# Layer 1 attention: the high and low halves of the queries stacked on the partitions

## The chip, the cores and the metric

The kernel runs on one core of one Trainium2 chip. The metric is the device time of one execution in microseconds (us). Before the change it is 1184.41 us, the median of three runs (1181.78 to 1184.94). The profile used below was taken of one further execution, which took 1183.15 us.

The engines are named as the profile names them: PE is TensorE (matrix products), PEld its loading of weights, DVE is VectorE, ACT is ScalarE, POOL is GpSimd and SP is SyncE, which issues the DMAs.

## The reference

Two decoder layers over 512 tokens of width 1024 in float32. Each layer has an attention mixer and a SwiGLU feed-forward block, both behind an RMS norm that is scaled and shifted by a condition. The change touches the mixer of layer 1 alone: sliding-window attention with 16 query heads of 64 elements, 4 key heads, a window of 128 and one learned sink per head. Cut to that:

```
q, k, v = _split_cols(h @ w_in, ODD_SIZES)              # 16 x 64, 4 x 64, 4 x 64
q = _rms_norm(q.reshape(b, s, C_HEADS, HEAD_DIM), qn_c)
k = _rms_norm(k.reshape(b, s, C_KV_HEADS, HEAD_DIM), kn_c)
...
logits = einsum('bnqhgd,bnkhd->bnhgqk', qb, kk) * HEAD_DIM ** -0.5   # band: own and previous block
logits = logits - slope * dist                                       # masked outside the window
p = softmax(concatenate([logits, sink]))[..., :-1]
out = einsum('bnhgqk,bnkhd->bnqhgd', p, vv)
```

The tokens are worked in four blocks of 128 queries. A block sees its own and the previous block's keys, 256 in all; block 0 sees only its own 128.

## The kernel before

Nearly all products run in the number type that the kernel calls FR, in which an operand is carried as two tiles: `hi`, a rounded copy, and `lo`, what the rounding left out. A product of two such operands is three matrix products into one accumulator: hi by hi, hi by lo and lo by hi (`mm3`). Every instruction is issued through a few helpers, so the profile's lines are those of the helpers: L434 is every matrix product (`mms`), L445 every transpose on PE (`tr`), L460 every ACT pass (`act`, `copy`), L476 every DVE or POOL operation on two tensors (`tt`), L496 the fused pass that scales the logits, adds the distances and takes the row minimum (`ttmin`), and L484 a multiplication by a scalar.

The order of the work is not the order of the code. Each helper hands an operation, with an estimate of its duration, to a list scheduler (`Sched`), which places the operations of all engines by dependencies, free buffers and priority; in up to eight rounds it sets new due times for DVE and keeps the shortest plan. The instructions are then emitted in that order, and each engine works through its own list in order. One call of `mms` is one operation for the scheduler: its products stand next to each other. For an FR product of n columns the estimate is 0.4219 ns times n, at least 107 ns, whatever part of the array it uses.

Layer 1 goes through `odd`. One chunk of weights gives keys and values. The keys of each of the 4 key heads are transposed to tiles `ckT` of 128 partitions by 512 tokens, and the head's 64 rows stand in them twice, in partitions 0 to 63 and again in 64 to 127. Then, for two groups of 8 query heads (`hg`), the four blocks of queries are projected (`proj_f`, 24 products of 512 columns with weights and activations in FR), normalised and transposed (`q_t`), and attended (`attn_c`). A transposed query tile has 4 column groups of 128 queries; each holds an even head in partitions 0 to 63 and the odd head beside it in 64 to 127. `split_out` makes of it the tiles `hi` and `lo` with one ACT pass and one DVE pass over 128 x 512.

`attn_c` makes the logits head by head: three products with 64 rows, in the head's own half of the partitions. The tiles of logits are PSUM buffers of the tag `lg`, two at a time besides what the scheduler grants as next in line, and `ttmin` on DVE empties them. The scheduler fills the gaps of the attention with the projections of the following blocks, and of the output product at the end.

Of the kernel before, what the change touches and what calls it, by code (L numbers as in the profile page):

```python
# [10 lines left out]
F = mybir.dt.float32  # L11
FR = mybir.dt.float32r
AF = mybir.ActivationFunctionType
OP = mybir.AluOpType
# [3 lines left out]
P = 128  # L18
# [22 lines left out]
def f32(v):  # L41
    return float(np.float32(v))
# [330 lines left out]
class Kern:  # L373
# [442 lines left out]
            self.copy(hi, src, scale=gain)  # L816
            self.stt(lo, src, gain, hi.bitcast(F), OP.mult, OP.subtract)

    def q_t(self, ps, qs):

        qf = self.t2("qf")
        r = self.head_rstd(ps, 8)
        self.tt(r, r, qs, OP.mult, e="POOL")
        self.tt(qf.rearrange("p (h d) -> p h d", d=64), ps.rearrange("p (h d) -> p h d", d=64),
                r[:, :, None].to_broadcast([P, 8, 64]), OP.mult)
        tp = self.ps("tp")
        for j in range(4):
            self.tr(tp[:, j * P:(j + 1) * P], qf[:, j * P:(j + 1) * P])
        hi, lo = self.t2("q", dt=FR), self.t2("q", dt=FR)
        self.split_out(tp, hi, lo)  # L830
        return [t.rearrange("p (a b) -> p a b", a=4) for t in (hi, lo)]


# [120 lines left out]
    def attn_c(self, i, hg, q, Y):  # L954

        b0 = max(i - 1, 0)
        nb = i + 1 - b0
        n = nb * P
        dsl = self.Dc[:, 256 - n:256]
        nm, sums, rec, es = (self.sm() for _ in range(4))  # L960
        pv = self.ps("pv")
        T = []
        for hp in range(4):
            t = self.t2("L")
            for e in range(2):
                h = 2 * hp + e
                r = slice(64 * e, 64 * e + 64)
                kh, kl = self.ckT[(8 * hg + h) // 4]
                ks = slice(b0 * P, b0 * P + n)
                lg = self.logits(q[0][r, hp], q[1][r, hp], kh[r, ks], kl[r, ks], n)  # L970
                self.ttmin(t[:, e * 256:e * 256 + n], lg[:, :n], dsl, f32(SL_C[8 * hg + h]), nm[:, h:h + 1])
                T.append((t, e * 256))
        hs = slice(8 * hg, 8 * hg + 8)
        self.tt(nm, nm, self.nsink[:, hs], OP.min)
        self.tt(es, nm, self.sinks[:, hs], OP.add, e="POOL")
        self.act(es, es, AF.Exp)
        for h, (t, c) in enumerate(T):
            self.act(t[:, c:c + n], t[:, c:c + n], AF.Exp, scale=-1.0, bias=nm[:, h:h + 1], accum=sums[:, h:h + 1])
        self.tt(sums, sums, es, OP.add)
        self.recip(rec, sums)  # L980
        for h, (t, c) in enumerate(T):
            self.ts(t[:, c:c + n], t[:, c:c + n], rec[:, h:h + 1], None, OP.mult)
        self.pv_t(pv, T, [[(t, c + b * P) for t, c in T] for b in range(nb)],
                  [tuple(self.cv[b0 + b][:, (2 * hg + g) * 64:(2 * hg + g) * 64 + 64] for g in range(2)) for b in range(nb)])
        self.y_out(pv, Y, i)
# [109 lines left out]
    def odd(self, H):  # L1095
        self.ckT = [(self.t2("k", dt=FR), self.t2("k", dt=FR)) for _ in range(4)]
        self.cv = []
        w = self.chunk()
        for i in range(NB):
            ps = self.proj_f(H, i, w, 512, "st")  # L1100
            t = self.t2("v")
            self.copy(t[:, 0:256], ps[:, 256:512])
            self.cv.append(t)
            r = self.head_rstd(ps[:, 0:256], 4)
            qf = self.k_t(ps[:, 0:256], r[:, 0:4], 4, True)
            tp = self.ps("tp")
            for j in range(4):
                self.tr(tp[:, j * P:(j + 1) * P], qf[:, j * P:(j + 1) * P])
            sl = slice(i * P, (i + 1) * P)
            for j in range(4):  # L1110
                self.split_out(tp[:, j * P:(j + 1) * P], self.ckT[j][0][:, sl], self.ckT[j][1][:, sl], self.gain[:, 2:3])
        ys = []
        for hg in range(2):
            w = self.chunk()
            Y = self.new_y()
            for i in reversed(range(NB)):
                ps = self.proj_f(H, i, w, 512)
                q = self.q_t(ps, self.qs[:, 16 + 8 * hg:24 + 8 * hg])
                self.attn_c(i, hg, q, Y)
            ys += Y  # L1120
        return ys
# [253 lines left out]
```

## Time and profile before

| | before |
|---|---|
| median of three runs | 1184.41 us |
| profiled execution | 1183.15 us, its span 1181.3 us |
| busy PE / PEld / DVE / ACT / POOL | 1158.7 / 995.8 / 903.3 / 604.6 / 85.3 us |
| mean granted clock of PE | 0.996 |
| PE in the chain that ended last | 86% |
| attention of layer 1, about 690 to 800 us from the start | 110 us |

The span runs from the first to the last instruction; 1.85 us lie around it. A busy time is the time in which at least one instruction of an engine runs. For PE it says little: the ends of matrix products are modelled, a product of 256 columns is listed with about 0.28 us although the next one starts 0.11 us later. What PE takes for a piece of work is therefore read from the starts of its instructions. In the names of forms, `64*128 64x256` is a product with 64 rows and 128 columns of weights and an operand of 256 columns that streams by; `128*128` uses all rows.

### The profile page before, as it was taken

Reading aid. Unit: us, or ns where it says so; the run is one execution under the profiler, and the core shown is the slowest. Engines: PE = TensorE matmul, PEld = TensorE weight load, DVE = VectorE, ACT = ScalarE, POOL = GpSimd, SP = SyncE. Lnnn points to the kernel's source line nnn. Section 1 sums busy time; section 2 is a strip of 40 time slices with the busy share of each in tenths; the row PEclk is TensorE's granted clock in tenths of the full one; section 3 lists DMA queues with packets and bytes.
Section 4 is the critical chain, followed back from the end, with each engine's and each line's share of the span. In section 5 each row is a group of like instructions: output and inputs, shape, how many; then the busy total and the mean of one; then the engine's idle time right before and its main releaser. Section 6 shows DMA issues by size and latency. Waiting matters only on the chain.

```text
span 1181.3 us, 19707 instructions
## 1 busy us (share of the span) xinstructions
PE 1158.7 (98%) x7648; PEld 995.8 (84%) x7648; DVE 903.3 (76%) x1976; ACT 604.6 (51%) x1396; POOL 85.3 (7%) x224
## 2 busy tenths in 40 slices
PE   6989999999999999999999999999999999999998
PEld 3867677679989988899989876668999988999988
DVE  6589999846998889889984866756999843788831
ACT  5564266854745522355533647664856521556510
POOL 0132223300000000000000111100000000000000
PEclk9999999999999999999999999999999999999999
DMA  9634614202244469634362231112123332133411
GB/s 350 247 135 175 220 68 146 72 1 72 72 170 151 162 235 334 250 143 148 138 234 105 72 107 37 72 37 72 72 80 103 139 125 72 72 108 108 161 37 36
DMA packets 32430, 151.78 MB, mean 128 GB/s; under 512 B 3152, under 2 KB 4304, under 8 KB 21072
## 3 DMA queue, kind: packets, MB, share of 16 engines
q1 hardware_dynamic: 32336, 150.52, 35.8%
q8 instruction: 60, 0.98, 0.3%
q14 instruction: 34, 0.28, 0.1%
HBM read 148.41 MB, written 2.10 MB: 127 GB/s over the span
## 4 chain that ended last, share of the span: by engine, by line
PE 86%; DVE 5%; ACT 1%; POOL 0%; issue 0%
PE ps L434 82%; PE ps L445 3%; DVE t L911 1%; DVE t L491 1%; DVE sm L910 1%; DVE w L476 1%; ACT t L460 0%; DVE t L476 0%; POOL sm L476 0%; DVE t L496 0%; DVE sm L502 0%; DVE t L484 0%; ACT sm L460 0%; POOL sm L484 0%; DVE sm L491 0%
## 5 line engine op out<-in xcount | busy, mean ns | idle before, releaser
L434 PE MATMUL ps<-t,w 128*128 128x256 f32 (+2 forms) x5520 | 821.5, 310 | 0.5 <-ACT t L460 0.4
L434 PEld LDWEIGHTS ps<-t,w 128*128 128x128 f32 x5520 | 751.9, 191 | 57.5 <-issue 6.2
L460 ACT ACTIVATE w<-raw 128x512 fp32r<-128x512 f32 (+1 forms) x364 | 225.3, 663 | 160.7 <-PE ps L434 92.6
L476 DVE TENSOR_TENSOR w<-raw,w 128x512 fp32r<-128x512 f32 (+1 forms) x340 | 244.6, 749 | 58.0 <-PE ps L434 43.0
L460 ACT ACTIVATE t<-ps 128x256 f32<-128x256 f32 (+6 forms) x376 | 151.0, 430 | 206.6 <-PE ps L434 145.7
L434 PE MATMUL ps<-w,t 128*128 128x512 f32 (+1 forms) x768 | 189.4, 390 | 0.1
L434 PEld LDWEIGHTS ps<-w,t 128*128 128x128 f32 x768 | 133.3, 190 | 35.2 <-issue 9.7
L476 DVE TENSOR_TENSOR t<-t,t 128x256 f32<-128x256 f32 (+3 forms) x159 | 81.6, 538 | 16.1 <-ACT t L460 15.7
L476 DVE TENSOR_TENSOR t<-ps,t 128x256 f32<-128x256 f32 (+4 forms) x188 | 73.7, 415 | 23.1 <-ACT t L460 12.2
L491 DVE SCALAR_TENSOR_TENSOR x<-ps,mod,x 128x512 f32<-128x512 f32 (+1 forms) x64 | 39.4, 615 | 66.2 <-PE ps L434 65.9
L434 PE MATMUL ps<-t,t 64*128 64x256 f32 (+5 forms) x592 | 86.2, 356 | 1.0 <-ACT t L460 0.5
L434 PEld LDWEIGHTS ps<-t,t 64*128 64x128 f32 (+2 forms) x592 | 56.0, 186 | 32.4 <-issue 18.2
L491 DVE SCALAR_TENSOR_TENSOR t<-raw,cond,t 128x512 f32<-128x512 f32 x112 | 77.8, 746 | 0.0
L445 PE MATMUL ps<-cst,t 128*128 128x128 f32 x388 | 62.2, 281 | 9.3 <-DVE t L476 7.1
L460 ACT ACTIVATE t<-t 128x512 fp32r<-128x512 f32 (+3 forms) x105 | 54.2, 528 | 31.8 <-DVE t L476 31.4
L460 ACT ACTIVATE t<-t,sm 128x256 f32<-128x256 f32 (+3 forms) x128 | 65.5, 515 | 9.1 <-DVE sm L496 7.4
L445 PEld LDWEIGHTS ps<-cst,t 128*128 128x128 f32 x388 | 45.5, 142 | 29.0 <-ACT t L460 7.0
L496 DVE CUSTOM_DVE_ANT_0 t<-ps,cst 128x256 f32<-128x256 f32 (+3 forms) x104 | 39.2, 408 | 25.4 <-PE ps L434 25.1
L460 ACT ACTIVATE w<-w 128x1024 fp32r<-128x1024 f32 x34 | 36.1, 1060 | 32.6 <-PE ps L434 25.2
L484 POOL TENSOR_SCALAR sm<-sm 128x8 f32<-128x8 f32 (+2 forms) x64 | 16.7, 261 | 476.7 <-DVE sm L502 456.8
L476 DVE TENSOR_TENSOR w<-w 128x1024 fp32r<-128x1024 f32 x34 | 41.5, 1220 | 10.9 <-PE ps L434 10.8
L476 DVE TENSOR_TENSOR w<-raw 128x1024 f32<-128x1024 f32 x34 | 41.5, 1221 | 10.1 <-PE ps L434 9.8
(74 smaller groups left out, 605.4 us busy)
## 6 DMA issues: line engine op xcount, KB each, us to landing
raw<-in_wg SPq DMA_DIRECT2D x44, 1024.0 KB, 4.8
raw<-in_ada SPq DMA_DIRECT2D x40, 1024.0 KB, 5.4
raw<-in_wd SPq DMA_DIRECT2D x20, 1024.0 KB, 4.8
raw<-in_w0c SPq DMA_DIRECT2D x10, 1024.0 KB, 6.5
t<-in_ada SPq DMA_DIRECT2D x32, 256.0 KB, 6.5
raw<-in_wo SPq DMA_DIRECT2D x8, 1024.0 KB, 4.9
raw<-in_w1c SPq DMA_DIRECT2D x6, 1024.0 KB, 4.9
x<-in_x SPq DMA_DIRECT2D x8, 256.0 KB, 4.5
```

The lines of the kernel that those rows point to most:

```text
L434: self.nc.tensor.matmul(o.ap(), l.ap(), r.ap(), start=st, stop=sp, skip_group_check=True)
L445: self.s.op("PE", 107, lambda: self.nc.tensor.transpose(out.ap(), src.ap(), self.ident.ap()), [out], [src, self.ident])
L460: self.nc.scalar.activation(out.ap(), src.ap(), func, **kw)
L476: lambda: self.eng(e).tensor_tensor(out.ap(), a.ap(), b.ap(), op=op), [out], [a, b])
L484: self.eng(e).tensor_scalar(out.ap(), a.ap(), val(s1), val(s2), op0=op0, **kw)
L491: lambda: self.eng(e).scalar_tensor_tensor(out.ap(), a.ap(), val(s), b.ap(), op0=op0, op1=op1),
L496: lambda: self.nc.vector.tensor_tensor_reduce(out.ap(), a.ap(), b.ap(), op0=OP.add, op1=OP.min, scale=scale, scalar=3e38, accum_out=accum. ...
L910: self.s.op("DVE", 65 + 1.05 * n, lambda m8=m8: self.nc.vector.max(m8.ap(), sc.ap()), [m8], [sc])
L911: self.s.op("DVE", 65 + 1.05 * n, lambda m8=m8: self.nc.vector.match_replace(sc.ap(), m8.ap(), sc.ap(), -3e38), [sc], [m8, sc])
```

## The change

With `stack=True`, which only layer 1 asks for, `q_t` no longer makes a tile of high and a tile of low parts. The first tile holds the even heads, high parts in partitions 0 to 63 and low parts in 64 to 127; the second holds the odd heads, high parts in 64 to 127 and low parts in 0 to 63. Each tile takes one ACT pass over 64 partitions and one DVE pass that reads 64 partitions and writes the other 64. Since the keys stand twice in `kh`, one product over all 128 rows gives hi by hi plus lo by hi; a second product with 64 rows adds hi by lo of the keys. A head has two products in place of three.

```
-    def q_t(self, ps, qs):
+    def q_t(self, ps, qs, stack=False):
...
-        self.split_out(tp, hi, lo)
+        if stack:
+
+            a, b = slice(0, 64), slice(64, P)
+            for t, u, v in ((hi, a, b), (lo, b, a)):
+                self.copy(t[u], tp[u])
+                self.tt(t[v], tp[u], t[u].bitcast(F), OP.subtract)
+        else:
+            self.split_out(tp, hi, lo)
...
-                lg = self.logits(q[0][r, hp], q[1][r, hp], kh[r, ks], kl[r, ks], n)
+                lg = self.ps("lg")
+                self.mms([(lg[:, :n], q[e][:, hp], kh[:, ks], True, False), (lg[:, :n], q[e][r, hp], kl[r, ks], False, True)])
...
-                q = self.q_t(ps, self.qs[:, 16 + 8 * hg:24 + 8 * hg])
+                q = self.q_t(ps, self.qs[:, 16 + 8 * hg:24 + 8 * hg], True)
```

On PE, at the first block of layer 1's attention, the rows before are these; t_7673 and t_7683 are the tiles `hi` and `lo` of a key head, t_7924 and t_7931 those of the queries:

```order
L434 MATMUL ps<-w,t_7427 128x512 x2
L434 MATMUL ps<-w,t_7452 128x512
L434 MATMUL ps<-t_7673,t_7924 128x256
L434 MATMUL ps<-t_7683,t_7924 128x256
L434 MATMUL ps<-t_7673,t_7931 128x256
L434 MATMUL ps<-t_7673,t_7924 128x256
L434 MATMUL ps<-t_7683,t_7924 128x256
L434 MATMUL ps<-t_7673,t_7931 128x256
```

All six have 64 rows: the first three are an even head, the last three the odd head beside it. In the same place the changed kernel has these, t_7924 being now the tile of the even heads and t_7931 that of the odd ones:

```order
L434 MATMUL ps<-w,t_7427 128x512 x2
L434 MATMUL ps<-w,t_7452 128x512
L434 MATMUL ps<-t_7673,t_7924 128x256
L434 MATMUL ps<-t_7683,t_7924 128x256
L434 MATMUL ps<-t_7673,t_7931 128x256
L434 MATMUL ps<-t_7683,t_7931 128x256
```

Each product with t_7673 has 128 rows and each with t_7683 has 64, so the two forms alternate; the projection in front stands where it stood. On DVE, at the split of the same block's queries, the rows before are these (the row without a tile reads the row minimum out):

```order
L502 TENSOR_REDUCE sm<-t_7917 128x8
L476 TENSOR_TENSOR t_7931<-ps,t_7924 128x512
L496 ISA t_7957,sm<-ps,cst 128x256
L496 ISA sm 128x1
L496 ISA t_7957,sm<-ps,cst 128x256
```

and in the changed kernel, where t_7959 is the tile of logits that was t_7957:

```order
L502 TENSOR_REDUCE sm<-t_7917 128x8
L476 TENSOR_TENSOR t_7924<-ps,t_7924 64x512
L476 TENSOR_TENSOR t_7931<-ps,t_7931 64x512
L496 ISA t_7959,sm<-ps,cst 128x256
L496 ISA sm 128x1
L496 ISA t_7959,sm<-ps,cst 128x256
```

One pass over 128 partitions becomes two over 64. Up to this place the order on PE is the same in both kernels; behind it the same work stands in a different interleaving until the attention ends. The DMAs on SP keep their order throughout.

## Rows read from the trace of the kernel before

**Rows 1.** The page, part 1: engine, busy us, share, instructions.
```profile
PE 1158.7 (98%) x7648; PEld 995.8 (84%) x7648; DVE 903.3 (76%) x1976; ACT 604.6 (51%) x1396; POOL 85.3 (7%) x224
```

**Rows 2.** Busy time by engine, attention of layer 1: stretch, length, PE, PEld, DVE, ACT, POOL, clock.
```profile
690.00:800.00 110.00, 108.30 (x629) 74.57 (x628) 72.33 (x288) 72.19 (x241) 12.42 (x53) 1.00 0.11 39
```

**Rows 3.** Chain of waits, 690 to 800: shares, then start us, length, what.
```profile
by line: PE ps L434 80.1%; PE ps L445 16.5%; DVE t L496 1.4%; ACT t L460 1.1%; DVE t L476 0.8%; issue 0.3%; DVE sm L496 0.0%
...
794.81 0.61 ACT t L460
```

**Rows 4.** Groups by form, 690 to 800: count, busy us, mean ns, idle before.
```profile
L434 PE MATMUL ps<-t,t 64*128 64x256 f32 x144 | 16.3, 305 | 0.2 <-DVE sm L496 0.2
...
L434 PE MATMUL ps<-t,t 64*128 64x128 f32 x48 | 5.5, 289 | 0.0
...
L496 DVE CUSTOM_DVE_ANT_0 t<-ps,cst 128x256 f32<-128x256 f32 x48 | 18.4, 420 | 12.5 <-PE ps L434 12.3
...
L476 DVE TENSOR_TENSOR t<-ps,t 128x512 fp32r<-128x512 f32 x8 | 5.4, 684 | 0.2 <-ACT t L460 0.2
...
L460 ACT ACTIVATE t<-ps 128x512 fp32r<-128x512 f32 x8 | 4.7, 598 | 7.9 <-PE ps L445 7.9
```

**Rows 5.** Timeline of PE, 687 to 699: start us, length, instructions.
```profile
687.53 5.73 PE L434 MATMUL ps<-w,t 128*128 128x512 f32 x24
693.11 0.60 PE L445 MATMUL ps<-cst,t 128*128 128x128 f32 x4
...
696.40 2.11 PE L434 MATMUL ps<-t,t 64*128 64x256 f32 x24
```

**Rows 6.** Timeline of PE, 699 to 706.
```profile
701.50 0.62 PE L434 MATMUL ps<-t,t 64*128 64x256 f32 x6
702.06 0.96 PE L434 MATMUL ps<-w,t 128*128 128x512 f32 x3
702.95 0.63 PE L434 MATMUL ps<-t,t 64*128 64x256 f32 x6
```

**Rows 7.** The same, in slits that catch single products.
```profile
701.18 0.40 PE L434 MATMUL ps<-w,t 128*128 128x512 f32 x1
...
701.73 0.40 PE L434 MATMUL ps<-t,t 64*128 64x256 f32 x4
...
702.39 0.40 PE L434 MATMUL ps<-w,t 128*128 128x512 f32 x1
```

**Rows 8.** Timeline of PE, slits about 738: one head alone.
```profile
738.11 0.38 PE L434 MATMUL ps<-t,t 64*128 64x256 f32 x1
...
738.34 0.39 PE L434 MATMUL ps<-t,t 64*128 64x256 f32 x2
...
738.45 0.27 PE L434 MATMUL ps<-t,t 64*128 64x256 f32 x1
738.65 0.33 PE L445 MATMUL ps<-cst,t 128*128 128x128 f32 x1
```

**Rows 9.** Timeline of PE, slits about 258, in layer 0.
```profile
258.34 0.38 PE L434 MATMUL ps<-t,w 128*128 128x256 f32 x1
...
258.56 0.40 PE L434 MATMUL ps<-t,w 128*128 128x256 f32 x2
...
258.68 0.28 PE L434 MATMUL ps<-t,w 128*128 128x256 f32 x1
258.89 0.33 PE L434 MATMUL ps<-t,t 64*128 64x128 f32 x1
```

**Rows 10.** Timeline of PE, 785 to 787: the last run.
```profile
785.53 0.55 PE L434 MATMUL ps<-t,t 64*128 64x128 f32 x3
786.01 1.19 PE L434 MATMUL ps<-t,w 128*128 128x512 f32 x4
```

**Rows 11.** Timeline, 690 to 700: the DVE split of block 3.
```profile
694.54 0.68 DVE L476 TENSOR_TENSOR t<-ps,t 128x512 fp32r<-128x512 f32 x1
```

## The prediction

> **What bounds the kernel now.** I read the page's busy times first, to see which engine could set the end: PE, with 98% of the span; DVE and ACT stand far below it [rows 1]. Then the same for the stretch in which layer 1 attends, 690 to 800 us: PE 108.3 of 110 us, DVE and ACT 72 each, the granted clock at 1.00, which is the upper of its two levels, 2.4 GHz [rows 2]. Then the chain of waits over that stretch: 96.6% of it is PE's own work, 3.7 us are waits for DVE, ACT and small steps, the longest at 794.8 us where the last block is finished [rows 3]. So what PE needs for the logits goes into the total at nearly its full size, and DVE or ACT work counts only where it comes late for PE.
>
> The groups by form show the work in question: 144 products of 256 columns and 48 of 128, all with 64 rows [rows 4]: three for each of 64 heads (16 heads in four blocks; 48 of the 64 see 256 keys, 16 see 128). How long PE takes for one is read from starts, in the timeline.
>
> **What a 64-row product costs.** Within a run of them, PE overlaps the even head with the odd one: 24 products of 8 heads take 2.1 us [rows 5], which is under 0.09 us each although a few of them wait. Of six products the last four start at 701.73 and the projection behind them at 702.06 [rows 7]. One head alone does not have this: its three products start at 738.11, 738.34 and 738.45, the transpose behind them at 738.65, 0.54 us for half the work that two heads do in 0.56 us (701.50 to 702.06) [rows 6, 8]. So the pace inside a run is 0.11 to 0.12 us for a pair of products (0.56 less the 0.23 and 0.21 that the first and the last pair take, below; I use 0.11), and 0.115 us for a product without a partner (738.34 to 738.45, and 0.54 less 0.23 and 0.20).
>
> Each change of form costs more than the work. There are four pieces. Projections follow each other at 0.23 us (24 in 5.58 us, 687.53 to 693.11 [rows 5]).
> - The last projection before a run takes 0.32 us to the next start (701.18 to 701.50), 0.09 to 0.10 more [rows 6, 7].
> - The first 64-row product holds the second up by 0.23 us in place of 0.115: 0.11 more [rows 8].
> - The last one takes 0.20 us to the next start: 0.09 more [rows 8].
> - The first full-array product after the run takes 0.33 us in place of 0.23 (702.06 to 702.39): 0.10 more [rows 6, 7].
>
> Together 0.40 us for one visit to the 64-row form. As a check: a run of six with three projections repeats every 1.45 us (701.50 to 702.95); less three projections, 0.69, that is 0.76 us, against 0.40 + 3 x 0.11 = 0.73 from the pieces [rows 6].
>
> By the Trainium skill ("TensorEngine Tiling (Array Packing)", section "Tiling Modes"), a change of the tiling mode, unlike a change of tile within a mode, drains TensorE. It gives no price; this case's rows put 0.40 us on a visit. What the rule adds is that the price would hang on the change itself, not on how long the run is, which no run in this trace shows, since the shortest has three products.
>
> **The change part by part.** Before, the 64-row products stand in 31 runs, the first at 696.40 and the last at 785.53 [rows 5, 10], so PE pays 31 visits: 31 x 0.40 = 12.4 us. In them are 20 pairs of heads and 8 single heads of 256 columns, 20 x 0.33 + 8 x 0.35 = 9.4 us, and 6 pairs and 4 single heads of 128 columns at nearly the same pace, 6 x 0.31 + 4 x 0.34 = 3.2 us. Sum before: 25.0 us.
>
> After, every head is a 128-row product followed by a 64-row product, and the next thing is again a full-array product. So no two 64-row products stand together: the overlap of even and odd heads is gone, and there are 64 visits, not 31. The price of a 128-row product of 256 columns that stands between two 64-row ones is seen in layer 0, with weight tiles: the first after a run takes 0.22 us to the next (258.34 to 258.56), one in the flow 0.12 (258.56 to 258.68), the last before a run 0.21 (258.68 to 258.89) [rows 9]. A single one pays both: 0.12 + 0.10 + 0.09 = 0.31 us. A single 64-row product pays 0.115 + 0.11 + 0.09 = 0.31 us. A head of 256 columns: 0.62 us. For 128 columns: the last run, one head, takes 0.48 us for three products [rows 10]; less two in the flow at 0.115 that leaves 0.25 us for one alone, and I give the 128-row product the same: 0.50 us a head.
>
> After: 48 x 0.62 + 16 x 0.50 = 29.8 + 8.0 = 37.8 us. Difference on PE: 37.8 - 25.0 = **+12.8 us**.
>
> No run here has a single 64-row product between two 128-row ones, so this is bounded from both sides. From below: no price for the change at all, 0.12 + 0.115 = 0.235 us a head of 256 columns and 0.22 of 128: 11.3 + 3.5 = 14.8 us, 10.2 us less than before. From above: 0.62 us for the 128-column heads too, 39.7 us, +14.7. I take the sum from the visits, since all runs of three and more pay all four pieces.
>
> The split of the queries costs one more ACT pass (0.60 us) and one more DVE pass (0.68 us) for each of 8 blocks [rows 4], if a pass over 64 partitions takes as long as one over 128: its 512 columns are the same. That is 4.8 us on ACT and 5.5 us on DVE, beside 72 of 110 us on either [rows 2]. I cost it at nothing. What hides it is the projection of the next block, which PE works on meanwhile: in the first block the DVE pass ends at 695.22 [rows 11] and PE comes to the logits at 696.40 [rows 5], 1.18 us later. Queued behind the added DVE pass are the `ttmin` of the first logits, which cannot start before the products anyway. If the cover were gone, 8 x (0.60 + 0.68) = 10.2 us would come on top.
>
> Two effects of the slower logits go the other way. DVE takes about 0.42 us for one head's `ttmin` [rows 4], and PE now needs 0.62 us for a head, so PE no longer waits for a PSUM buffer in the long runs. And with PE later, the 3.7 us of other waits in the chain [rows 3] may shrink. I take nothing for them and leave 3.7 us in the range. The DMAs keep their order, and PE's order ahead of the attention is the same.
>
> Sum: against the profiled execution, 1183.15 us, 1183.15 + 12.8 = 1196.0. That execution lies 1.26 us below the median of the runs, 1184.41; put on the median it is 1197.2. I forecast 1197.
>
> **Rivals.**
> - *The weight loads hide.* If, with single products, the load of the next weights runs during the drain, the two pieces of 0.10 to 0.11 us behind a change go, and a head costs 0.21 + 0.20 = 0.41 us: 48 x 0.41 + 16 x 0.40 = 26.1 us, +1.1, so 1185.5, no change that can be told. For it: in the flow, loads are hidden entirely. Against it: every run read above pays these pieces, on both sides [rows 7 to 9]. By the Trainium skill ("TensorE: Matmul & The Clock Gate", "Architectural detail: the array is 16× 32×32, not 1× 128×128") a product can begin before its weight load completes, and TensorE's queue pulls loads ahead of products in flight; by that the time would be this rival's. The trace shows it in the flow and not across a change of form.
> - *Faster: the two products of a head go without a change.* They add into one buffer and the 64-row weights are a part of the 128-row weights before them. If PE then does not pay a visit, the lower bound holds: 1184.4 - 10.2 = 1174.2 us. It decides from where a visit costs less than (25.0 - 14.8) / 64 = 0.16 us. For it: two thirds of the products remain, and the estimates of the scheduler count it so. Against it: the products are of the form that pays in every run read here, whatever stands beside it, projections or transposes.
> - *The split comes late as well.* ACT and DVE are each the last step before the logits; if all 8 blocks waited, 1197.2 + 10.2 = 1207.4. Against it is the 1.18 us of slack and PE falling further behind.
>
> **How the numbers follow.** Forecast 0.78, between 1191 and 1203 (from 3.7 us of waits saved and a smaller visit, to the upper bound of +14.7 and a part of the split). Late split 0.09, hidden loads 0.08, no change of form 0.05. What a measurement of this kernel can tell from no change is 0.3%, 3.6 us. Slower by more: 0.78 + 0.09 and a sliver of the third case, 0.88; within it 0.07; faster 0.05. The range, 1188 to 1205, leaves out the faster case, most of the hidden loads and the far end of the late split.
>
> **What would show it.** Right: 64 products of form 128*128 and 64 of 64*128 in the logits, single 64-row products about 0.31 us before the next start, and the same after a 128-row one; the first 8 heads taking about 5 us in place of 2.1; the stretch to the end of the attention about 13 us longer; longer waits of `ttmin` for PE; the feed-forward part unchanged in length. Wrong: the two products of a head 0.12 us apart (faster or no change), or PE waiting for the DVE split ahead of the logits.

## The result, and the profile after

The changed kernel takes 1199.9 us, the median of four runs (1197.79 to 1201.21); the kernel before takes 1183.18 us beside it. The ratio is 1.0138, with a 95% interval of 1.0127 to 1.0150: slower by 15.0 to 17.7 us. Run again later on another occasion it came out at 1.0128 (1.0113 to 1.0143). The forecast was 1197 us, and the range of 1188 to 1205 holds the time. One execution among those of the experiments below, one of five of the version with all rows, took 3925 us and is left out of that version's ratio.

The page's first part, the row that answers to [rows 1]:

```profile
PE 1174.2 (98%) x7584; PEld 1005.2 (84%) x7584; DVE 910.6 (76%) x1984; ACT 608.9 (51%) x1404; POOL 85.5 (7%) x224
```

There are 64 products fewer on PE and 8 passes more on DVE and on ACT, as the change says, and PE is busy for 15.5 us longer. The attention of layer 1, by engine as in [rows 2], and the chain of waits over it as in [rows 3]:

```profile
690.00:813.00 123.00, 122.97 (x570) 84.00 (x568) 79.25 (x290) 76.97 (x248) 12.58 (x53) 0.99 0.07 26
```

```profile
by line: PE ps L434 85.8%; PE ps L445 14.3%; issue 0.0%
```

PE paced 96.6% of this stretch before, and paces all of it now: the waits for DVE and ACT are gone, and the stretch is longer all the same. The products of the logits, by form, beside [rows 4]:

```profile
L434 PE MATMUL ps<-t,t 64*128 64x256 f32 x48 | 18.3, 381 | 0.0
L434 PE MATMUL ps<-t,t 128*128 128x256 f32 x48 | 17.0, 355 | 0.0
...
L434 PE MATMUL ps<-t,t 64*128 64x128 f32 x16 | 5.2, 324 | 0.0
L434 PE MATMUL ps<-t,t 128*128 128x128 f32 x16 | 4.8, 297 | 0.0
```

They alternate, one of each for a head. The first block on PE, beside [rows 5] (a row that begins with a 128-row product holds the 64-row ones too, since the names are the same):

```profile
693.31 3.01 PE L434 MATMUL ps<-w,t 128*128 128x512 f32 x12
696.16 4.97 PE L434 MATMUL ps<-t,t 128*128 128x256 f32 x16
701.06 1.32 PE L434 MATMUL ps<-w,t 128*128 128x512 f32 x3
702.18 1.05 PE L445 MATMUL ps<-cst,t 128*128 128x128 f32 x4
702.89 3.25 PE L434 MATMUL ps<-w,t 128*128 128x512 f32 x9
```

Eight heads take 4.9 us to the next projection, 0.61 us each; before, 24 products took 2.1 us. Single products in the same run, seen through slits, answer to [rows 8, 9]; the last two rows are a head of 128 columns:

```profile
696.37 0.38 PE L434 MATMUL ps<-t,t 64*128 64x256 f32 x1
...
696.68 0.38 PE L434 MATMUL ps<-t,t 128*128 128x256 f32 x1
...
696.99 0.38 PE L434 MATMUL ps<-t,t 64*128 64x256 f32 x1
...
743.80 0.33 PE L434 MATMUL ps<-t,t 128*128 128x128 f32 x1
...
744.05 0.32 PE L434 MATMUL ps<-t,t 64*128 64x128 f32 x1
744.31 0.50 PE L434 MATMUL ps<-w,t 128*128 128x512 f32 x1
```

A 64-row product takes 0.31 us to the next start and so does the 128-row one between two of them; with 128 columns it is 0.25 to 0.26 for either.

One thing in the timeline was not forecast: behind the first block, projections and transposes are slow (three projections from 701.06, four transposes over 1.05 us where 0.60 was usual [rows 5]). Stretches of the changed kernel, with the granted clock as the third number from the end:

```profile
696.00:701.00 5.00, 5.00 (x18) 2.89 (x16) 3.73 (x16) 0.00 (x0) 0.60 (x3) 1.00 0.00 0
701.50:704.80 3.30, 3.30 (x12) 2.61 (x11) 0.40 (x3) 1.18 (x2) 0.00 (x0) 0.50 0.00 0
705.00:708.00 3.00, 3.00 (x13) 2.06 (x13) 2.26 (x8) 1.83 (x7) 0.20 (x1) 1.00 0.00 0
```

From 701.5 to 704.9 PE ran at the lower level of its clock, 1.2 GHz, and before that it had alternated between the two forms for 4.9 us at the full one. The kernel before has 1.00 through the whole attention [rows 2].

### The profile page after: what moved, and what is told of

Same layout as the page of the kernel before. It is cut to its first block, busy times and chain, and to the rows that moved or that the text cites. A ratio compares the mean times of both kernels' runs of the same rounds, so it can differ in the third digit from the quotient of the medians.

```text
span 1196.0 us, 19595 instructions
## 1 busy us (share of the span) xinstructions
PE 1174.2 (98%) x7584; PEld 1005.2 (84%) x7584; DVE 910.6 (76%) x1984; ACT 608.9 (51%) x1404; POOL 85.5 (7%) x224
## 4 chain that ended last, share of the span: by engine, by line
PE 88%; DVE 2%; DMA 0%; ACT 0%; POOL 0%; issue 0%; ACTq 0%
PE ps L434 85%; PE ps L445 3%; DVE t L491 1%; DVE w L476 1%; DMA raw<-in_ada 0%; DVE t L476 0%; POOL sm L476 0%; ACT t L460 0%; DVE t L496 0%; DVE sm L502 0%; DVE t L484 0%; DVE x L491 0%; ACT sm L460 0%; POOL sm L484 0%; DVE sm L491 0%
## 5 line engine op out<-in xcount | busy, mean ns | idle before, releaser
L460 ACT ACTIVATE t<-ps 128x256 f32<-128x256 f32 (+7 forms) x384 | 155.8, 434 | 223.5 <-PE ps L434 152.1
L434 PE MATMUL ps<-t,t 64*128 64x256 f32 (+6 forms) x528 | 103.3, 376 | 1.4 <-ACT t L460 0.8
L476 DVE TENSOR_TENSOR t<-ps,t 128x256 f32<-128x256 f32 (+5 forms) x196 | 79.9, 427 | 27.6 <-ACT t L460 16.8
L434 PEld LDWEIGHTS ps<-t,t 64*128 64x128 f32 (+2 forms) x528 | 64.0, 187 | 38.5 <-issue 16.8
L460 ACT ACTIVATE t<-t,mod 128x256 fp32r<-128x256 f32 (+2 forms) x72 | 37.5, 572 | 22.4 <-DVE t L491 22.2
```

The source lines that it names most:

```text
L434: self.nc.tensor.matmul(o.ap(), l.ap(), r.ap(), start=st, stop=sp, skip_group_check=True)
L460: self.nc.scalar.activation(out.ap(), src.ap(), func, **kw)
L476: lambda: self.eng(e).tensor_tensor(out.ap(), a.ap(), b.ap(), op=op), [out], [a, b])
```

## The experiments

Two theories were set against each other. **A:** every visit to the 64-row form costs about 0.40 us, and the changed kernel pays 64 of them in place of 31. **B:** the products are not it; the time goes to the split's added passes and to the new order of the work.

**All rows for the second product.** One edit, and no other instruction moves:

```
-                self.mms([..., (lg[:, :n], q[e][r, hp], kl[r, ks], False, True)])
+                self.mms([..., (lg[:, :n], q[e][:, hp], kl[:, ks], False, True)])
```

> The second product of each head takes all 128 rows of the query tile and of the low key tile, in place of 64 (it adds low by low, which the reference's value contains too); every engine's order, the split and the number of products are those of the changed kernel. Theory A (the loss is paid by visits to the 64-row form, about 0.40 us each): a head falls from 0.62 to about 0.24 us, 48 x 0.38 + 16 x 0.28 = 22.7 us less than the changed kernel, and the half-clock stretch behind the first block goes with it (1.7 us or more): 1173 to 1176 us, faster than before. Theory B (the loss is paid by the split's added passes and by the new order): about 1200, since both stay.

Measured: 1178.22 us against 1183.5 before, ratio 0.9953 (0.9937 to 0.9969). With the same number of products, the same order on every engine and the same split, the kernel is 21 us faster than the changed one; B is out. The first block:

```profile
696.35 2.18 PE L434 MATMUL ps<-t,t 128*128 128x256 f32 x16
698.36 0.86 PE L434 MATMUL ps<-w,t 128*128 128x512 f32 x3
```

Eight heads in 2.01 us, 0.25 us each, and no half clock behind them. It missed A's 1173 to 1176 by 2 to 5 us. The chain over 690 to 800 says what now stands beside PE:

```profile
by line: PE ps L434 76.2%; PE ps L445 14.0%; ACT t L460 5.1%; DVE t L476 2.0%; DVE t L496 1.7%; DVE sm L502 0.5%; issue 0.3%; DVE sm L476 0.2%; ACT sm L460 0.1%; DVE sm L496 0.0%
...
775.20 2.54 ACT t L460 x6
777.83 2.46 ACT t L460 x11
```

PE now paces 90% of the stretch. With the products cheap, the softmax on ACT ends last near the end of the attention.

**The split alone.** The kernel before, its three products untouched, with the split in halves:

```
...
-        self.split_out(tp, hi, lo)
+        for u in ((slice(0, 64), slice(64, P)) if halves else (slice(0, P),)):
+            self.split_out(tp[u], hi[u], lo[u])
...
```

> The kernel before, with its three 64-row products, but the split of layer 1's queries made in two ACT and two DVE passes over 64 partitions each, as many as in the changed kernel. Theory A: the passes lie beside PE's work: 1182 to 1186 us, no change. Theory B: several us slower than before, up to 10 us if PE waits for all of them.

Measured: 1183.8 us, ratio 1.0002 (0.9992 to 1.0011). The passes are there, 16 of 0.69 us on DVE:

```profile
L476 DVE TENSOR_TENSOR t<-ps,t 64x512 fp32r<-64x512 f32 x16 | 11.0, 688 | 2.2 <-ACT t L460 1.8
```

The whole kernel is not slower by anything that can be told. But the scheduler also made another order for it, from about 185 us on, so this run does not single out the split: from the first logits to the end its profiled execution takes 486.3 us (695.16 to 1181.45), 1.4 us more than the kernel before (484.9), and ahead of them 1.2 us less. That the passes lie beside PE's work in the changed kernel is shown by its own chain, in which PE has all of the stretch.

**Grouped and alternating pairs.** One operation for two heads, with two accumulators, in two orders of the same four products; both with `wo=5` in the list of PSUM limits:

```
...
-                self.mms([(lg[:, :n], q[e][:, hp], kh[:, ks], True, False), (lg[:, :n], q[e][r, hp], kl[r, ks], False, True)])
+            full = [(lgs[e][:, :n], q[e][:, hp], kh[:, ks], True, False) for e in range(2)]
+            half = [(lgs[e][:, :n], q[e][64 * e:64 * e + 64, hp], kl[64 * e:64 * e + 64, ks], False, True) for e in range(2)]
+            self.mms(full + half)      # the other run: [full[0], half[0], full[1], half[1]]
...
```

> The changed kernel with one PE operation for a pair of heads in the order 128-row, 128-row, 64-row, 64-row (and one PSUM buffer fewer for the output product, without which the planner finds no order). Theory A: 32 visits and the two 64-row products overlap: 32 x 0.40 + 24 x 0.35 + 8 x 0.32 = 23.8 us of PE in place of 37.9, so 12 to 14 us less than the pair in alternating order, about 1184. Theory B: within 2 us of the pair in alternating order.

> As the run with grouped pairs, but in the order 128-row, 64-row, 128-row, 64-row: 64 visits as in the changed kernel. Theory A: 1196 to 1201 us, 12 to 14 us more than grouped. In its plan no more than two heads stand together, so if the half-clock stretch of the changed kernel comes from its run of eight heads, the granted clock stays at 1.00 here and the time is 1196 to 1198. Theory B: the same time as grouped.

Measured: grouped 1198.68 us, ratio 1.0125 (1.0108 to 1.0141); alternating 1211.7 us, ratio 1.0248 (1.0218 to 1.0277). The two have the same order on every engine but for the four products. The difference between them, 13.0 us, is what A forecast for 32 visits and the lost overlap, and B had none. Both levels were missed, by 15 us and by 11 to 16 us, so the pairs cost something by themselves. Nor did the clock stay up in the alternating run. In its profiled execution, with 1218.39 us the longest of four (the others took 1210.23 to 1211.88):

```profile
772.50:789.50 17.00, 16.79 (x40) 9.73 (x39) 8.66 (x37) 8.98 (x35) 0.40 (x2) 0.50 0.06 25
864.70:868.10 3.40, 3.40 (x19) 3.40 (x18) 3.40 (x9) 2.55 (x7) 0.00 (x0) 0.50 0.00 0
```

The expectation that no more than two heads stand together does not hold: ahead of the longer stretch four do.

```profile
768.62 2.46 PE L434 MATMUL ps<-t,t 128*128 128x256 f32 x8
```

**The kernel before, in pairs.** To see what the pairs cost alone: the three 64-row products of two heads in one operation, again with `wo=5`.

```
...
-                lg = self.logits(q[0][r, hp], q[1][r, hp], kh[r, ks], kl[r, ks], n)
...
+                jobs += [(lgs[e][:, :n], q[0][r, hp], kh[r, ks], True, False), (lgs[e][:, :n], q[0][r, hp], kl[r, ks], False, False),
+                         (lgs[e][:, :n], q[1][r, hp], kh[r, ks], False, True)]
+            self.mms(jobs)
...
```

> The kernel before with its three 64-row products, but one PE operation for a pair of heads and one PSUM buffer fewer for the output product, as in the two runs with pairs. It tells why the grouped pair came out at 1198.7 us though it visits the 64-row form no oftener than the kernel before. If the plan with paired operations costs the time (and half-clock stretches 5.1 us of it), this run is about 1193 us. If mixing 128-row and 64-row products costs more than the visits, this run is about 1183.

Measured: 1189.17 us, ratio 1.0044 (1.0029 to 1.0059), between the two numbers: the plan with pairs costs 5.5 us, not 10. The grouped pair stands 9.5 us above it. In the profiled executions that is 8.0 us (spans 1195.8 and 1187.8). 2.6 us of it lie ahead of the attention, where the plans differ (first logits at 697.94 and 695.30); three half-clock stretches in place of one, 6.8 us more, are 3.0 us at the price found below; and the waits named for PE are 7.5 us in place of 4.9:

```profile
PE ps L445 <- DVE t L484: 3.6, 4, 1.3
PE ps L434 <- DVE t L476: 3.3, 2, 3.0
```

```profile
PE ps L445 <- DVE t L484: 3.7, 3, 1.7
PE ps L434 <- DVE t L491: 0.6, 1, 0.6
```

The first two rows are the grouped pair's longest waits of PE between 690 and 845 us, the others those of the kernel before in pairs. These pieces come to 8.2 us. The logits themselves, summed from start to start without the waits among them and with what they put on the instructions beside them, take 23.7 us in the grouped pairs (A had 23.8) and 22.9 in the kernel before in pairs. So a further cost of mixing the forms, if there is one, is about 1 us; all of this was read from one execution each.

**All rows in the first block alone, and the changed kernel again.** To separate the visits from the clock:

```
-                self.mms([..., (lg[:, :n], q[e][r, hp], kl[r, ks], False, True)])
+                u = slice(0, P) if i == 3 and hg == 0 else r
+                self.mms([..., (lg[:, :n], q[e][u, hp], kl[u, ks], False, True)])
```

> The changed kernel, but in the first block of the attention alone (eight heads in a row) the second product takes all 128 rows; every engine's order stays. Theory A (visits alone): 8 heads fall from 0.62 to 0.24 us, 3.0 us less than the changed kernel. Theory A with the clock: the run of eight alternating heads is also what lets the granted clock fall to half behind it, so that stretch goes too and with it 1.7 us more, 4.7 us in all, and the profile shows 1.00 between 700 and 706 us. Theory B (split and order): no change from the changed kernel.

> The changed kernel as it is, on the same chip as the run with the first block over all rows: 1198 to 1201 us, with at least one stretch of 3.4 us at half clock behind the first block of the attention.

Measured on one chip: 1195.6 us (ratio 1.0096, 1.0079 to 1.0113) and 1199.31 us (1.0128, 1.0113 to 1.0143), 3.7 us apart, between 3.0 for the visits alone and 4.7 with the clock. The profile decides against the second. The stretch at half clock has not gone but moved, from behind the first block to a later place:

```profile
696.00:699.00 3.00, 3.00 (x22) 2.72 (x21) 2.69 (x11) 0.00 (x0) 0.71 (x4) 1.00 0.00 0
699.00:706.00 7.00, 7.00 (x30) 4.91 (x29) 5.85 (x21) 5.26 (x18) 0.40 (x2) 1.00 0.00 0
735.20:738.60 3.40, 3.40 (x13) 2.78 (x14) 1.37 (x9) 0.62 (x2) 0.20 (x1) 0.50 0.00 0
```

From the first logits to the end of the span the two profiled kernels take 499.8 us (696.16 to 1196.0) and 497.0 us (696.31 to 1193.3): with one such stretch in each, 2.9 us apart, the eight heads' visits. So the run of eight heads is not what the clock needs to fall. The later place is the end of the next longest run, in which PE alternates over five heads:

```profile
732.22 3.29 PE L434 MATMUL ps<-t,t 128*128 128x256 f32 x10
```

The changed kernel's second profile gives the price of half clock, since the program is the same. It has three times as much of it:

```profile
699.30:706.10 6.80, 6.80 (x18) 5.07 (x18) 2.54 (x8) 1.19 (x2) 0.00 (x0) 0.50 0.00 0
740.30:743.70 3.40, 3.40 (x13) 3.02 (x13) 1.61 (x8) 0.93 (x3) 0.20 (x1) 0.50 0.00 0
```

The second of these stands behind the same five heads:

```profile
737.10 3.20 PE L434 MATMUL ps<-t,t 128*128 128x256 f32 x10
```

The half clock comes to 10.2 us in place of 3.4, and first logits to end take 502.8 us (695.41 to 1198.2), 3.0 us more: 0.44 us lost for each us at half clock, or 1.5 us for one stretch. The single runs agree in direction: the changed kernel's runs with a mean clock of 0.994 took 1197.6 to 1199.0 us, those at 0.991 to 0.993 took 1200.0 to 1201.2.

**A version that beats both.** All rows in layer 1, and the same in the second kind of attention of layer 0, whose one key head also stands twice in its tile.

```
...
-                lg = self.logits(q[0][r, h // 2], q[1][r, h // 2], self.bkT[0][r, :n], self.bkT[1][r, :n], n)
+                lg = self.ps("lg")
+                self.mms([(lg[:, :n], q[h % 2][:, h // 2], self.bkT[0][:, :n], True, False),
+                          (lg[:, :n], q[h % 2][:, h // 2], self.bkT[1][:, :n], False, True)])
...
-            q = self.q_t(ps, self.qs[:, 8:16])
+            q = self.q_t(ps, self.qs[:, 8:16], True)
```

> As the run with all rows in layer 1, and the same for the second kind of attention of layer 0 (8 heads against one key head that stands twice in its tile). Counted with the prices of this study, its products fall from 17.4 to 10.0 us on PE. Where PE sets the pace there: about 1171 us. Where VectorE does (it makes the selection in that stretch): as with layer 1 alone, 1178.

Measured: 1176.91 us, ratio 0.9938 (0.9923 to 0.9953), the lowest median of the study, but 1.3 us under layer 1 alone, not 7, and the intervals of the two ratios overlap. In the profiled executions the first logits of layer 1 come 1.0 us sooner (695.35 and 696.35), and what follows takes 479.9 us in both; two executions of the changed kernel, one program, differ by 0.75 us at that place (696.16 and 695.41). The chain from 200 to 262 us, first with layer 1 alone, then with both:

```profile
by line: PE ps L434 78.0%; PE ps L445 21.6%; DVE t L496 0.7%; issue 0.1%; DVE sm L496 0.0%
```

```profile
by line: PE ps L434 53.1%; PE ps L445 17.1%; ACT t L460 8.3%; DVE t L484 5.7%; DVE t L476 5.4%; DVE t L496 4.6%; DVE t L491 3.5%; issue 1.3%; DVE sm L491 0.8%; DVE sm L505 0.3%; DVE sm L496 0.1%
```

PE paced 99.6% of this stretch and then 70%: DVE and ACT stand in the chain for most of the rest, so most of what PE saved turned into waits for them.

## Why the prediction was right

- **The price of a visit.** Worked out from runs of three and more products, it held for single ones: 0.31 us for a 64-row and 0.31 for a 128-row product, 0.25 to 0.26 for either with 128 columns, against 0.31 and 0.25. This was the step without a row of its own, and the rival of hidden weight loads (0.41 us a head) falls with it. A run of a single product pays the whole visit, which the first trace could not show. This agrees with the Trainium skill ("TensorEngine Tiling (Array Packing)", section "Tiling Modes"), by which a change of the tiling mode drains TensorE.
- **The visits and the pairs.** 64 in place of 31 and no overlap of even and odd heads: +12.8 us forecast. Summed over all heads from start to start, without the waits among them and with what a visit puts on the instructions beside it, the logits take 24.7 us before and 38.6 us after, +13.9, where the forecast had 25.0 and 37.8. Five of the 64 heads are followed by a product with 64 columns of weights and not by a full-array one, as the prediction has it; that form uses all rows too, and the count of 64 visits stands. With the order of every engine held fixed, taking the 64-row products out shortens the profiled kernel by 19.9 us from the first logits to the end (499.8 to 479.9, from 696.35 to 1176.3); 1.5 us of that is half clock, so 18.4 us, where the visits had 22.7. ACT and DVE, which the chain then names, are where the rest would have gone, but the waits listed for PE behind the first logits rise by 0.9 us only (1.2 to 2.1), so it is not shown where all of the 4.3 us went. With the order of four products alone exchanged it is 13.0 us where the visits had 14.1.
- **The split.** Costed at nothing, and no cost of it shows: no pass of DVE or ACT is in the chain of the changed kernel's attention, and the kernel before with the split in halves, in another order, came out at 1.0002. The added passes take 0.59 and 0.69 us, as long as over 128 partitions, and the late split is no rival any more:

```profile
L460 ACT ACTIVATE t<-ps 64x512 fp32r<-64x512 f32 x16 | 9.5, 591 | 13.6 <-PE ps L445 13.4
```

- **Other waits.** The 3.7 us that I left in the range did go from the chain, but little time with them: the waits listed for PE behind the first logits are 1.2 us in place of 1.7. DVE now idles longer for PE ahead of `ttmin`, 16.3 us in place of 12.5 [rows 4], as forecast:

```profile
L496 DVE CUSTOM_DVE_ANT_0 t<-ps,cst 128x256 f32<-128x256 f32 x48 | 19.8, 422 | 16.3 <-PE ps L434 16.2
```

- **What was missing.** The profiled execution is 14.6 us longer than that of before (1197.79 against 1183.15), the forecast had 12.8. Half clock is 1.5 us of it, and more in the runs that have more of it: the medians stand 16.7 us apart. I had read 1.00 in the stretch and not asked what the change does to the clock; that is the term of the sum that was left out. The part behind the attention, which was to stay as it was, is 0.95 us longer: the new order brings PE one wait for DVE there, and so it does in the run with all rows.

```profile
845.03 2.17 PE L434 MATMUL ps<-t,w 128*128 128x256 f32 x16 [0.60 <-DVE t L491]
```

From the first logits to the end the two profiled executions are some 15 us apart (499.8 and 484.9). The logits' 13.9 and the 1.5 at half clock, less 0.5 of listed waits (the new one counted in), come to 14.9. A small part of the nearness is luck: beside the changed kernel the kernel before stood at 1183.18, not at the 1184.41 that the forecast started from, so 12.8 us of the 16.7 were forecast, though the time was missed by only 2.9.
- **The faster rival** was right about the count of products and wrong about PE: two thirds of the products pay only if none of them changes the form, which is the version with all rows. Even that one gave 5 us and not 10; its chain names ACT and DVE for a tenth of the stretch.

## What to carry to other kernels

Count the changes between a product form that uses part of the rows and one that uses all of them before counting the products; here a visit cost 0.40 us, more than three products of 256 columns. A product that would use half the rows of weights already stacked over all rows can be run over all rows, when the operand that streams by stands in both halves too: a 128-row product in the flow takes 0.12 us to the next start and a 64-row one 0.115 [rows 8, 9], and the version with all rows is some 21 us faster than the changed kernel. And when the products become cheaper, look at who stands right behind PE in the chain: of 22.7 and 7.4 us counted on PE, 18.4 and about 1 reached the end.

## What the runs showed of the hardware that was not expected

The granted clock fell to half, 1.2 GHz, in layer 1's attention or within 50 us behind it: for 3.4 and 10.2 us in two profiles of the changed kernel, 3.4 us with the first block changed, 10.2 us in the grouped pairs, 20.5 us in the alternating pairs and 3.4 us in the kernel before in pairs; not at all there in the one profile each of the kernel before, of the split alone and of the two versions with all rows.

By what PE did ahead of them, the falls are of two kinds. All three of the grouped pairs, the one near 794 us of the kernel before in pairs and the one at 864.7 us of the alternating pairs stand in or soon behind waits of PE for DVE, of 0.7 to 3.0 us. The kernel before has such falls too, ahead of layer 1's attention, at 72.6 and 144.3 us, with waits of 2.2 and 2.3 us. One row each of the kernel before, of its version in pairs and of the grouped pairs, with the wait in brackets:

```profile
143.93 1.26 PE L445 MATMUL ps<-cst,t 128*128 128x128 f32 x6 [2.26 <-DVE t L476]
792.16 1.12 PE L445 MATMUL ps<-cst,t 128*128 128x128 f32 x4 [1.67 <-DVE t L484]
842.94 1.22 PE L434 MATMUL ps<-t,ones 128*128 128x256 f32 x2 [2.98 <-DVE t L476]
```

The others, those of the changed kernel, of the run with the first block changed and the stretch of 17 us in the alternating pairs, have no wait of more than 0.21 us close ahead. PE had alternated between the two forms over eight, five or four heads in a row, and it counted as busy all the while; ahead of 701.5 us it had done nothing else for 4.9 us. Neither is always followed by a fall. PE waits 1.3 us at 809 us in the grouped pairs without one, and the changed kernel's first profile has the same five heads at 736.5 to 739.6 us and a clock of 1.00 behind them. What else it takes is open.
